# A transformer block's opening: the order of the first transfers, a column copy moved to another engine, and one more filling product

## The chip, the cores and the metric

The kernel runs on one core of one Trainium2 chip. The metric is the time of one execution on the device in microseconds (us), as the median of three runs. Besides the runs there is one execution that was taken with the hardware profiler; all rows below come from it.

## The reference, cut to what matters

The block takes x (512 rows of 1024 numbers), puts 16 meta rows ahead of it, normalizes every row, and projects the result with a wide matrix; two kinds of attention, gates, a merge and an output projection follow. The change touches only the first step and the transfers that stand beside it:

```python
h = jnp.concatenate([meta, x], axis=1)
h = layer_norm(h, emb_ln_g, emb_ln_b)
...
proj = jnp.einsum('bld,dn->bln', h, w_in[i])
```

`layer_norm` takes a row's mean and variance, then multiplies column by column by `emb_ln_g` and adds `emb_ln_b`. `b_gate` and `diff_subln_g` are small vectors that are used much later (a bias of the gates, the scale of a second norm).

## The kernel before, in words

The 512 rows of x are four tiles of 128 rows (`xts[0]` to `xts[3]`, here tile 0 to tile 3); the meta rows are a tile `mt` of 16 rows. For each tile the vector engine (DVE) takes statistics of the two halves of 512 columns (`stats`, line 323), joins them (line 327), and a reciprocal root follows: on ScalarE (ACT) for tile 0 (lines 329, 330), on GpSimd (POOL) for the others (lines 299, 300). DVE then writes the normalized tile (`norm_v`, line 340), except for the second half of tile 0, which ACT writes (`norm_s`, line 337). TensorE (PE) turns the tile by eight 128x128 transposes (`turn`, line 344). ACT scales and shifts each turned piece by the columns of `emb_ln_g` and `emb_ln_b` (`scaled`, line 384; two pieces of tile 0 go to DVE, line 386). As soon as a piece is there, PE multiplies it with the first weights (`query`, line 390: `x..` is the first weight block `raw0[:, 0]`, `y..` the second, `raw0[:, 1]`).

The columns themselves come from a transpose of 16 rows, `cp` (line 313), which PE makes after a run of filling products (`fill(WARM)`, lines 307 to 311; one filling product is two passes in the trace). The copy of `cp` out of PSUM into `cols` is line 415, in `norm0`, and it stands on ACT.

The order of the work of PE, DVE, ACT and POOL in this opening is written out by hand as a string and then pinned engine by engine (`keep_order`, line 970), so each engine does its work in the order of the text. Its first words are (`S` = statistics, `N` = normalize, `t` = turn, `F` = fill, `a` and `d` = scale on ACT and DVE):

```python
    def norm0():
        norm_v(0, X0)
        norm_s(0, X1)
        s.copy(cols[:, :16], av0[:, :16])
...
    order("""S0 norm0 t00 t01 t02 t03 S1 F2 a00 a01 a02 a03 a04 a05 d06 d07 x00 x01 x02 x03 x04 x05 N1 t10 t11 x06 x07 t12 t13
             a10 a11 a12 a13 a14 a15 a16 a17 S2 m0 m1 mr N2 S3 mnorm
             x10 y00 x11 y01 x12 y02 x13 y03 t20 more t21 t22 t23 x14 y04 x15 y05 x16 y06 x17 y07
```

The transfers into the chip are issued from SyncE (SP) in the order of lines 257 to 271: the halves of tile 0, the halves of tile 1, the two halves of the first weight block (`first_load`, line 133), tile 2, the second weight block, the meta rows, tile 3, the third weight block, `b_gate` and `diff_subln_g` into `rows2`, the fourth weight block, `diff_lambda`, and then the weights of the main part (`fetch`, line 145). The two vectors of the norm come on ACT's queue (lines 249, 250). Each transfer reports through a semaphore; SP has eight of them in turn, so a request waits until the one that last used its semaphore has landed.

Of the kernel before, what the change touches and what calls it, by code (L numbers as in the profile page):

```python
# [16 lines left out]
P = 128  # L17
# [17 lines left out]


ORDERED = [mybir.EngineType.PE, mybir.EngineType.DVE, mybir.EngineType.Activation, mybir.EngineType.Pool]
WARM = 12
SEVEN = 4
SUMS_AT = {0: [8.0], 1: [5.0, 11.0], 2: [8.0]}  # L40
TD = [(0.85, 11.0, 14.5), (0.95, 13.0, 16.5)]
# [5 lines left out]
def hybrid_block_kernel(ctx: ExitStack, tc: tile.TileContext, x, meta, emb_g, emb_b, w_in, b_gate,  # L47
                        diff_lambda, subln_g, w_br_d, w_br_s, w_out, ln_g, ln_b, out):
    nc = tc.nc
    v, s, g, pe = nc.vector, nc.scalar, nc.gpsimd, nc.tensor  # L50
# [22 lines left out]
    for u, (kind, n) in enumerate(UNITS):  # L73
        if u + 1 < len(UNITS):
            other, i = UNITS[u + 1]
# [15 lines left out]
    for n, (kind, i) in enumerate(seq):  # L91
        if kind in ("BD", "BS", "wd", "ws"):
# [6 lines left out]
            o = len(loads)  # L99
# [31 lines left out]
    def first_load(n, ks=slice(0, KT)):  # L131
        kind, i = seq[n]
        nc.sync.dma_start(raw0[:, n, ks], w_in[:, ks, ds(COL[kind] + i * P, P)])
# [118 lines left out]
    xts = [sp.tile([P, D], F32, name=f"xt{i}") for i in range(NB)]  # L252
# [1 line left out]
    mt = sp.tile([P, D], F32, name="mt")[:M]  # L254
    small = sp.tile([P, 512], F32, name="small")
    rows2, lamb = small[:17, :P], small[:, P:P + 256].rearrange("p (a d) -> p a d", a=4)
    for i in range(2):
        for o in (ts(0, 512), ts(1, 512)):
            nc.sync.dma_start(xts[i][:, o], x[0, ts(i, P), o])
    first_load(0, ts(0, 4))  # L260
    first_load(0, ts(1, 4))
    nc.sync.dma_start(xts[2], x[0, ts(2, P), :])
# [1 line left out]
    nc.sync.dma_start(mt, meta)  # L264
    nc.sync.dma_start(xts[3], x[0, ts(3, P), :])
    first_load(2)
    nc.sync.dma_start(rows2[0:16], b_gate[0].rearrange("a (k p) -> (a k) p", p=P))
    nc.sync.dma_start(rows2[16:17], subln_g)
    first_load(3)
    nc.sync.dma_start(lamb, diff_lambda[0].rearrange("a d -> (a d)").partition_broadcast(P))  # L270
    fetch(4)
# [14 lines left out]
    cols = const.tile([P, 33], F32, name="cols")  # L286
# [20 lines left out]
    def fill(count):  # L307
        for n in range(count):
            pe.matmul(warm, ident, ident, start=True, stop=True)

    fill(WARM)
    av0 = pav.tile([P, 512], F32, tag="av", name="cp")
# [23 lines left out]
    def norm_s(i, o):  # L336
        s.activation(xns[i][:, o], xts[i][:, o], AF.Identity, scale=xrs[:, i:i + 1], bias=nmr[i])

    def norm_v(i, o):
        v.tensor_scalar(xns[i][:, o], xts[i][:, o], xmv[:, i, 0:1], xrs[:, i:i + 1], op0=ALU.subtract, op1=ALU.mult)  # L340
# [71 lines left out]
    def norm0():  # L412
        norm_v(0, X0)
        norm_s(0, X1)
        s.copy(cols[:, :16], av0[:, :16])

    def mnorm():
        v.tensor_scalar(mn, mt, mmv[:, 0:1], mrs, op0=ALU.subtract, op1=ALU.mult)
# [33 lines left out]
    def lam2():  # L452
# [6 lines left out]
    steps["F"] = fill  # L459
    steps["H"], steps["L"] = lambda n, c: hi(2 * n + c), lambda n, c: lo(2 * n + c)  # L460
    words = dict(lam0=lam0, lam1=lam1, lam2=lam2, hm=lambda: s.copy(hTh[:, :, :M], hM), lm=low_meta, norm0=norm0, mnorm=mnorm, mturn=mturn, meta=meta, more=more_banks,
                 m0=lambda: stats(4, 0), m1=lambda: stats(4, 1), mr=lambda: rstd(4))

# [814 lines left out]
```

## Time and profile before

| | |
|---|---|
| median of three runs | 705.79 us (705.67 to 706.04) |
| the profiled execution's own time | 705.09 us |
| its span in the trace | 703.3 us |
| PE busy | 693.3 us, 99% of the span |
| DVE, ACT, POOL busy | 569.5, 440.5 and 129.8 us |

A row of a timeline gives the start and the length of a group of instructions from the start of the span, and in brackets how long its engine had been idle before it and who ended that idle time. `PEld` is the loading of the stationary operand of a matmul, which comes just ahead of the matmul. `SPq` and `ACTq` rows are the issue of a transfer, not the transfer. Matmul lengths overlap, since PE is pipelined: what counts for pace is the distance from one start to the next.

### The profile page before, as it was taken

How to read it: one execution, taken by the hardware profiler on the slowest of the kernel's cores; microseconds unless marked ns; L12 is line 12 of the kernel's file. 1: busy time of each engine (PE TensorE's matmuls, PEld its weight loads, DVE VectorE, ACT ScalarE, POOL GpSimd, SP SyncE). 2: the span in 40 equal slices, each digit the busy share in tenths (PEclk: the TensorE clock that was granted, in tenths of full speed). 3: DMA queues.
4: the chain of work that ended last, by engine and by line, in shares of the span. 5: the costliest groups of instructions: out<-in, count | busy, mean ns of one | idle time of the engine just before them, and what ended most of it. 6: DMA issues, size and time to landing. Idle time of an engine off the chain costs nothing.

```text
span 703.3 us, 13282 instructions
## 1 busy us (share of the span) xinstructions
PE 693.3 (99%) x4478; PEld 634.1 (90%) x4478; DVE 569.5 (81%) x1225; ACT 440.5 (63%) x1073; POOL 129.8 (18%) x140
## 2 busy tenths in 40 slices
PE   8999999999999999999999999999999999999996
PEld 8999999989899898999989899988888998999885
DVE  6887998878786777899887898977666888688887
ACT  6676767767566687777757687766555456555400
POOL 2243112222222201212121220000012201230011
PEclk9999999999999999999999999999999999999999
DMA  9399557988888796899898977547477749697702
GB/s 292 103 195 182 145 117 178 212 177 184 221 186 182 188 195 183 173 223 206 207 192 219 203 152 194 164 124 242 137 165 142 148 121 245 136 174 194 264 25 116
DMA packets 184215, 124.93 MB, mean 178 GB/s; under 512 B 8994, under 2 KB 168131, under 8 KB 184147
## 3 DMA queue, kind: packets, MB, share of 16 engines
q1 hardware_dynamic: 148050, 102.84, 50.5%
q0 software_dynamic: 35776, 20.19, 23.0%
q10 hardware_dynamic: 320, 1.06, 0.4%
q8 instruction: 35, 0.57, 0.3%
q14 instruction: 34, 0.27, 0.1%
HBM read 93.54 MB, written 9.44 MB: 146 GB/s over the span
## 4 chain that ended last, share of the span: by engine, by line
PE 93%; ACT 2%; SPq 1%; DVE 1%; DMA 1%; issue 0%; DVEq 0%; ACTq 0%
PE q L700 18%; PE ps L501 12%; PE ps L499 12%; PE ps L500 12%; PE q L1083 11%; PE pso L1206 6%; PE ps L515 6%; PE sc L764 6%; PE t L776 4%; PE tv L733 1%; PE av L931 1%; PE av L932 1%; DMA raw<-in_w_in_dram 1%; PE av L925 1%; PE av L933 1%; DMA xt<-in_x_dram 1%
## 5 line engine op out<-in xcount | busy, mean ns | idle before, releaser
L190 DVE TENSOR_TENSOR w<-raw,w 128x512 fp32r<-128x512 f32 x168 | 114.3, 689 | 37.7 <-ACT w L185 36.4
L500 PE MATMUL ps<-hTl,w 128*128 128x512 f32 x368 | 144.9, 394 | 0.0
L499 PE MATMUL ps<-hTh,w 128*128 128x512 f32 x368 | 144.7, 393 | 0.0
L501 PE MATMUL ps<-hTh,w 128*128 128x512 f32 x368 | 144.7, 393 | 0.0
L185 ACT CAST w<-raw 128x512 fp32r<-128x512 f32 x168 | 103.5, 627 | 11.6 <-PE ps L501 5.4
L147 POOL DMA_DIRECT2D rawk<-in_w_in_dram x48 | 66.1, 1630 | 119.5 <-DMA rawk<-in_w_in_dram 66.1
L700 PE MATMUL q<-tS,w 128*128 128x264 f32 x384 | 82.6, 289 | 0.0
L1083 PE MATMUL q<-gh,w 128*128 128x256 f32 x448 | 81.4, 283 | 0.2 <-ACT t L1092 0.2
L501 PEld LDWEIGHTS ps<-hTh,w 128*128 128x128 f32 x368 | 69.2, 188 | 13.5
L500 PEld LDWEIGHTS ps<-hTl,w 128*128 128x128 f32 x368 | 69.2, 188 | 13.1
L499 PEld LDWEIGHTS ps<-hTh,w 128*128 128x128 f32 x368 | 69.2, 188 | 13.0
L1083 PEld LDWEIGHTS q<-gh,w 128*128 128x128 f32 x448 | 70.2, 192 | 0.5 <-ACT t L1092 0.4
L764 PE MATMUL sc<-k,A 128*128 128x264 f32 (+3 forms) x320 | 66.0, 299 | 0.0
L700 PEld LDWEIGHTS q<-tS,w 128*128 128x128 f32 x384 | 63.7, 189 | 0.3
L1083 PE MATMUL q<-gl,w 128*128 128x256 f32 x224 | 63.5, 283 | 0.0
L700 PE MATMUL q<-hTh,w 128*128 128x264 f32 x288 | 60.8, 286 | 0.0
L916 DVE TENSOR_TENSOR_SCAN e<-e,diag 128x528 f32<-128x528 f32 (+1 forms) x64 | 54.2, 850 | 5.6 <-ACT e L910 5.6
L700 PE MATMUL q<-tl,w 128*128 128x264 f32 x192 | 54.9, 286 | 0.0
L764 PEld LDWEIGHTS sc<-k,A 128*128 128x128 f32 x320 | 50.1, 189 | 2.2
L515 PE MATMUL ps<-hTh,w 128*128 128x264 f32 x256 | 51.5, 289 | 0.2 <-ACT k L642 0.2
L700 PEld LDWEIGHTS q<-hTh,w 128*128 128x128 f32 x288 | 47.8, 189 | 1.0
L781 ACT CAST ah<-t 128x384 fp32r<-128x384 f32 (+2 forms) x72 | 34.3, 477 | 21.7 <-PE t L776 21.6
(284 smaller groups left out, 1572.1 us busy)
## 6 DMA issues: line engine op xcount, KB each, us to landing
raw<-in_w_in_dram SPq DMA_DIRECT2D x142, 256.0 KB, 3.4
rawk<-in_w_in_dram POOLq DMA_DIRECT2D x48, 256.0 KB, 5.7
rawk<-in_w_in_dram SPq DMA_DIRECT2D x36, 256.0 KB, 4.1
k<-ks SPq DMA_DIRECT2D x60, 132.0 KB, 3.0
raw<-in_w_out_dram SPq DMA_DIRECT2D x16, 256.0 KB, 4.0
k<-ks SPq DMA_DIRECT2D x60, 66.0 KB, 2.7
A<-low SPq DMA_DIRECT2D x28, 128.0 KB, 3.1
raw<-in_w_br_diff_dram SPq DMA_DIRECT2D x12, 256.0 KB, 3.3
```

The source lines that it names most:

```text
L147: second[l] = [lambda raw=raw, x=x: g.dma_start(raw, x, accum_op=ALU.add) for x in more]
L185: s.copy(wh, raw)
L190: eng.tensor_tensor(wl, raw, wh.bitcast(F32), op=ALU.subtract)
L499: pe.matmul(ps, wh[:, k % 4, :], hTh[:, k, M:], start=(k == 0), stop=False)
L500: pe.matmul(ps, wh[:, k % 4, :], hTl[:, k, M:], start=False, stop=False)
L501: pe.matmul(ps, wl[:, k % 4, :], hTh[:, k, M:], start=False, stop=(k == KT - 1))
L515: pe.matmul(ps[:, :H2], a[:, k % 4, :], b[:, k, ts(c, H2)], start=(k == 0 and m == 0), stop=(k == KT - 1 and m == 2))
L700: pe.matmul(bank, a[:, k, :], b, start=start and k == 0 and j == 0, stop=k == 3 and j == 2, skip_group_check=not start)
L764: pe.matmul(ps[:, :n], q, K[:, m, k0:k0 + n], start=(m == 0), stop=(m == 1))
L916: v.tensor_tensor_scan(rev, rev, diag[0][:, L - nk:][:, ::-1], 0.0, ALU.mult, ALU.max)
L1083: pe.matmul(bank, a[:, k, :], b[:, n, k, :], start=start and k == 0 and m == 0, stop=k == 3 and m == 2, skip_group_check=not start)
L1206: pe.matmul(ps, MH[k][:, ts(t, P)] if m == "h" else ML[:, k, ts(t, P)], WO[c]["hl".index(w)][:, k, r], start=(n == 0), stop=(n == 3 * KT - 1))
```

## The change

`WARM` goes from 12 to 13. Tile 1 is requested as a whole by one transfer in place of two halves. The requests for `b_gate` (16 rows of 128 numbers, 8 KB) and `diff_subln_g` (0.5 KB) move from behind the third weight block to a place ahead of the first weight block. The copy of the 16 columns goes from ACT to DVE, where it stands behind the normalization of tile 0's first half and ahead of the statistics of tile 1.

```diff
-WARM = 12
+WARM = 13
...
-    for i in range(2):
-        for o in (ts(0, 512), ts(1, 512)):
-            nc.sync.dma_start(xts[i][:, o], x[0, ts(i, P), o])
+    for o in (ts(0, 512), ts(1, 512)):
+        nc.sync.dma_start(xts[0][:, o], x[0, ts(0, P), o])
+    nc.sync.dma_start(xts[1], x[0, ts(1, P), :])
+    nc.sync.dma_start(rows2[0:16], b_gate[0].rearrange("a (k p) -> (a k) p", p=P))
+    nc.sync.dma_start(rows2[16:17], subln_g)
     first_load(0, ts(0, 4))
     first_load(0, ts(1, 4))
     nc.sync.dma_start(xts[2], x[0, ts(2, P), :])
@@
     nc.sync.dma_start(mt, meta)
     nc.sync.dma_start(xts[3], x[0, ts(3, P), :])
     first_load(2)
-    nc.sync.dma_start(rows2[0:16], b_gate[0].rearrange("a (k p) -> (a k) p", p=P))
-    nc.sync.dma_start(rows2[16:17], subln_g)
     first_load(3)
@@
     def norm0():
         norm_v(0, X0)
         norm_s(0, X1)
-        s.copy(cols[:, :16], av0[:, :16])
+        v.tensor_copy(cols[:, :16], av0[:, :16])
```

## Rows read from the trace of the kernel before

**Rows 1.** The page: busy time by engine; the chain that ended last.

```profile
PE 693.3 (99%) x4478; PEld 634.1 (90%) x4478; DVE 569.5 (81%) x1225; ACT 440.5 (63%) x1073; POOL 129.8 (18%) x140
...
PE 93%; ACT 2%; SPq 1%; DVE 1%; DMA 1%; issue 0%; DVEq 0%; ACTq 0%
```

**Rows 2.** Busy time by stretch: length, PE, PEld, DVE, ACT, POOL, clock, DMA share, GB/s.

```profile
5.97:7.15 1.18, 0.00 (x1) 0.00 (x1) 0.72 (x3) 0.86 (x3) 0.00 (x0) 1.00 1.11 342
...
10.27:26.27 16.00, 16.00 (x120) 15.02 (x118) 15.11 (x45) 13.93 (x38) 3.04 (x6) 1.00 0.68 210
...
34.00:703.30 669.30, 662.12 (x4257) 604.62 (x4255) 543.97 (x1156) 418.16 (x1015) 121.93 (x113) 1.00 0.75 177
```

**Rows 3.** Who waited for whom, on PE: us in total, times, longest.

```profile
PE bank L344 <- DVE xn L340: 1.2, 1, 1.2
```

**Rows 4.** Timeline of DVE, 0 to 22 us.

```profile
3.71 0.69 DVE L323 BATCH_NORM_STATS2 lnst<-xt 128x6 f32<-128x512 f32 x1 [1.91 <-DMA xt<-in_x_dram]
4.83 0.69 DVE L323 BATCH_NORM_STATS2 lnst<-xt 128x6 f32<-128x512 f32 x1 [0.43 <-DMA xt<-in_x_dram]
...
6.43 0.21 DVE L332 TENSOR_SCALAR nmr<-xmv,xrs 128x1 f32<-128x1 f32 x1 [0.66 <-ACT xrs L330]
6.56 0.54 DVE L340 TENSOR_SCALAR xn<-xt,xmv,xrs 128x512 f32<-128x512 f32 x1
7.01 1.28 DVE L323 BATCH_NORM_STATS2 lnst<-xt 128x6 f32<-128x512 f32 x2
...
9.54 1.00 DVE L340 TENSOR_SCALAR xn<-xt,xmv,xrs 128x512 f32<-128x512 f32 x2 [0.40 <-POOL xrs L300]
...
21.39 0.28 DVE L430 TENSOR_TENSOR hM<-bank,cols 128x128 f32<-128x128 f32 x1
21.71 0.29 DVE L431 TENSOR_TENSOR hM<-hM,cols 128x128 f32<-128x128 f32 x1
```

**Rows 5.** Timeline of PE's weight loads, 0 to 12 us; the last from 11.7 to 11.75.

```profile
7.15 0.85 PEld L344 LDWEIGHTS bank<-ident,xn 128*128 128x128 f32 x8 [1.27 <-DVE xn L340]
...
8.42 1.82 PEld L390 LDWEIGHTS bank<-hF,raw 128*128 128x128 f32 x12
10.15 0.47 PEld L344 LDWEIGHTS bank<-ident,xn 128*128 128x128 f32 x4
...
11.59 0.30 PEld L390 LDWEIGHTS bank<-hF,raw 128*128 128x128 f32 x2
```

**Rows 6.** Timeline of ACT, 0 to 22 us.

```profile
0.74 0.59 ACTq L249 DMA_DIRECT2D rows<-in_emb_ln_g_dram  x1
...
7.40 0.15 ACT L415 COPY cols<-cp 128x16 f32<-128x16 f32 x1
7.69 2.20 ACT L384 ACTIVATE hF<-bank,cols 128x128 f32<-128x128 f32 x6
```

**Rows 7.** Timeline of SP's queue, 0 to 22 us.

```profile
0.74 1.82 SPq L259 DMA_DIRECT2D xt<-in_x_dram  x4
2.60 0.98 SPq L133 DMA_DIRECT2D raw<-in_w_in_dram  x2
...
4.18 0.43 SPq L133 DMA_DIRECT2D raw<-in_w_in_dram  x1
4.82 2.36 SPq L264 DMA_DIRECT2D mt<-in_meta_tokens_dram  x1
...
8.16 1.94 SPq L267 DMA_DIRECT2D small<-in_b_gate_dram  x1
10.14 0.31 SPq L268 DMA_DIRECT2D small<-in_diff_subln_g_dram  x1
```

**Rows 8.** Issues around 2.3, 3.3 and 4.4 us: size, us from issue to landing.

```profile
xt<-in_x_dram SPq DMA_DIRECT2D x1, 256.0 KB, 5.0
...
raw<-in_w_in_dram SPq DMA_DIRECT2D x1, 256.0 KB, 5.5
...
raw<-in_w_in_dram SPq DMA_DIRECT2D x1, 512.0 KB, 7.4
```

## The prediction, made before the changed kernel was run

> **What bounds the kernel now.** I read the page first. PE is busy for 693.3 of 703.3 us, and the chain that ended last is 93% PE [rows 1]: what the opening does to the time is what it does to the moment from which PE runs without a gap. So I looked for that moment in the table of stretches [rows 2]. From 5.97 to 7.15 us PE does nothing; from 10.27 to 26.27 it is busy for 16.00 of 16.00 us; behind 34 us for 662.12 of 669.30. A delay ahead of 10.27 us therefore goes through to the end nearly whole, and a gain too, since hardly any idle time is left to take it up. The list of waits says the same: behind the first filling products, PE waits long in the opening only once, 1.2 us for the normalized first half of tile 0 [rows 3].
>
> The next step is what sets 10.27 us. PE's loads [rows 5] show the first six products in twelve loads from 8.42 us, and then at 10.15 us the first transpose of tile 1. That transpose has two conditions: the sixth product ahead of it in PE's order, and DVE's normalized half of tile 1. DVE writes that half from 9.54 us, 0.54 us for a half by tile 0's row, so until 10.08 us [rows 4]. Tile 0 shows how long the hand-over to PE takes: the half ends at 6.56 + 0.54 = 7.10 us and PE loads at 7.15. So 10.08 plus 0.05 is 10.13, and PE loads at 10.15: DVE's chain has no slack worth the name here, and neither have the products. The chain back from there is DVE's and POOL's: the half waited 0.40 us for POOL's root, POOL for the statistics of tile 1, and these started at 7.01 us directly behind tile 0's half, with no idle time noted [rows 4].
>
> **The change, part by part.**
>
> *One filling product more* is two passes. Eight loads take 0.85 us [rows 5], some 0.11 us from one to the next, so it adds 0.22 us to PE ahead of the transpose of the columns. PE is idle from 5.97 to 7.15 us [rows 2], which hides it; without that cover it would cost its 0.22 us. The columns would be there at about 6.2 us, and the copy can't start on DVE before 7.0. The granted clock is 1.00 in that stretch, the higher of the two levels, so there is no lower clock to be avoided. Zero.
>
> *The column copy leaves ACT.* It ran from 7.40 to 7.55 us, and the first scaled piece started at 7.69 [rows 6]. That piece also needs the first two transposes, which were loaded from 7.15 us [rows 5]. So ACT gains between 0 and 0.15 us, and I take 0.05. It reaches PE as a sixth product that ends sooner by as much. But the transpose behind it has its other condition at 10.13 us, and that one does not come sooner. The gain is hidden: zero.
>
> *The column copy goes to DVE*, behind tile 0's half and ahead of the statistics of tile 1. Queued behind it are the statistics, the joining, POOL's root, the normalization of tile 1 and the transposes. The trace has no such copy on DVE. The lower bound is a small instruction on operands outside PSUM: from 6.43 to 6.56 us, 0.13 us from start to start. The upper bound is an instruction that reads 128 columns from PSUM: from 21.39 to 21.71 us, 0.32 us [rows 4]. Sixteen columns are nearer to the small one; with a little for the PSUM read I take 0.15 us. The copy's own input has long been there, so it adds no wait. No gain is possible from this item, as DVE has no idle time there to fall into.
>
> [...]
>
> *Tile 1 requested whole.* SP saves one issue, 1.82 / 4 = 0.46 us [rows 7]. The fourth request was issued at about 0.74 + 3 x 0.47 = 2.15 us and landed 5.0 us later, at 7.1 [rows 7, 8]. Before, the first statistics needed only the third request; now they need the whole tile. The bytes and their place in the queue are the same, so I take 7.1 again. DVE comes to them at 7.01 + 0.15 = 7.16 us, so there is 0.06 us of slack. Landing sooner gains nothing, as DVE is busy; landing later costs its lateness. Zero, with a small margin.
>
> *The small requests ahead of the first weights.* Issuing 8 KB with nothing queued should cost SP what ACT's first request of 4 KB cost, 0.59 us at most [rows 6], and the 0.5 KB took 0.31 [rows 7]. Less the saved 0.46 us the first weights are issued up to 0.44 us later; I take 0.25. Their second half was issued at 2.60 + 0.48 = 3.08 us and landed 5.5 us later, at 8.6 [rows 7, 8]. Its first user is the fifth product, the ninth of the twelve loads from 8.42 to 10.24, at about 9.6 us [rows 5]. A slack of 1.0 us covers it. The second weight block is tighter: issued at 4.18, landed 7.4 us later, at 11.6 [rows 7, 8], and needed by the second load of the pair from 11.59, after the two of a first-weight product, at 11.70 [rows 5]. With DVE's delay it is needed at 11.85. The DMA engines are full meanwhile (share 1.11 at 342 GB/s, [rows 2]), so it lands by the bytes ahead of it: 8.5 KB more are 0.025 us. By bytes it lands at 11.63, by issue at 11.85, both in time. Zero.
>
> *Behind the third weight block* SP loses two issues, 1.94 and 0.31 us [rows 7]. The fourth block and the rest are then requested up to 2.3 us sooner. Nothing in PE's gapless 16 us waited for them, so that is worth nothing.
>
> **The sum** is +0.15 us, with 0.13 and 0.32 as the bounds of its one term. Against the profiled execution it is 705.09 + 0.15 = 705.24. That execution was 0.70 us below the median of the runs, so on the runs' scale I forecast 705.79 + 0.15 = 705.94, given as 705.9. A measurement of this kernel can tell about 0.2% from no change, 1.41 us: faster is below 704.38, slower above 707.20. So the forecast is no change that can be told.
>
> **The rivals.**
>
> *A: tile 0 lands sooner.* DVE waited 0.43 us for the second half of tile 0 and 1.91 us for the first [rows 4]. Fewer, larger requests behind it could let the second half through sooner. For it: these waits are on the path, ahead of everything. Against it: both requests stand ahead of every changed one in SP's order. Full success on the second half gives 0.15 - 0.43 = -0.28, 705.5 us. With some of the 1.91 us as well the gain could pass 1.41.
>
> *B: tile 1 lands later as a whole.* It decides from 7.16 us on, microsecond for microsecond. If the whole lands 0.5 us later than its second half did, the time is 705.79 + 0.15 + 0.44 = 706.4 us. For it: the slack is 0.06 us. Against it: same bytes, same place.
>
> *C: the small requests carry their long issue with them*, and the weights come late: the slower side. The two slow issues in the list are small ones, 2.36 us for 64 KB and 1.94 us for 8 KB [rows 7]. If 1.94 is the price of such a request wherever it stands, the weights are issued 1.94 + 0.31 - 0.46 = 1.8 us later. Where they land by issue, the second weight block lands at 11.6 + 1.8 = 13.4 instead of 11.6, and PE, which needs it at 11.70, stands for 1.7 us: 705.79 + 1.7 = 707.5 us, slower by 0.24%. It decides from a landing behind 11.85 us. For it: both rows. Against it: both stood directly behind a 512 KB request with more than 1 MB under way, whereas the 0.5 KB request took 0.31 and ACT's 0.59; and the engines were full, so that a later issue must not mean a later landing.
>
> *D: the copy costs nothing after all*, since the hand-over to the next instruction overlaps. Then nothing moves: 705.8 us.
>
> **How the numbers follow.** The forecast, with its bounds up to 0.32 us, has a chance of 0.60; A 0.14, most of it at a few tenths; B 0.11; C 0.10, of which 0.07 passes 1.41 us; D 0.05. Beyond 1.41 us faster there is only the far end of A, 0.03. So faster 0.03, slower 0.07, same 0.90. The range reaches from A's 705.5 less what the runs scatter (0.12 and 0.25 us about their median), 705.2, to B's 706.4 plus the same and a little for C's lighter forms, 706.8. Left out are C's full price and A's far end, under 2 in 10.
>
> **What would show it.** Right: a DVE copy of some 0.15 us from start to start at about 7.0 us; the statistics of tile 1 at 7.1 to 7.2; the first transpose of tile 1 at about 10.3; PE without a gap from there; the fill and the transpose of the columns done by 6.3 us. The step on ACT is right if its first piece starts hardly before 7.65 us. Wrong: an idle time of DVE ahead of tile 1's statistics that a transfer ended (B); statistics of tile 0 that start before 3.7 or 4.8 us (A); a long issue of `b_gate` at 2.1 us and PE waiting for weights at 8.4 or 11.7 us (C). A time outside 705.2 to 706.8 with this opening intact would mean that the order of later transfers changed the main part, which nothing in these rows lets me price.

## The result, and the profile after

The kernel after takes 706.62 us, median of its runs (705.85 to 707.72), the kernel before 705.76 beside it (704.66 to 706.30). The ratio is 1.0015, 95% interval 1.0009 to 1.0021: slower by 1.06 us by the ratio (0.86 by the two medians). That is less than the 1.41 us that the prediction took as what can be told, but the interval lies wholly above 1. The forecast was 705.9, in the range 705.2 to 706.8. The profiled execution took 706.10 us with a span of 704.3; that of before took 705.09 with 703.3, so the two traces differ by the same 1.0 us.

The page of the kernel after, as in [rows 1], and two stretches, as in [rows 2]; the last line is the second of these in the kernel before.

```profile
PE 694.4 (99%) x4480; PEld 635.0 (90%) x4480; DVE 570.5 (81%) x1226; ACT 440.7 (63%) x1072; POOL 129.8 (18%) x140
```

```profile
10.27:26.27 16.00, 16.00 (x118) 15.01 (x118) 15.12 (x45) 13.87 (x38) 3.04 (x6) 1.00 0.66 202
26.27:34.00 7.73, 7.18 (x56) 6.82 (x55) 5.26 (x13) 3.27 (x10) 3.06 (x10) 1.00 0.28 82
```

```profile
26.27:34.00 7.73, 7.51 (x59) 7.17 (x58) 5.21 (x13) 3.58 (x11) 3.12 (x10) 1.00 0.28 79
```

PE is gapless from 10.27 us in both. Then the kernel after loses 0.33 us against the kernel before between 26 and 34 us (7.18 us busy in place of 7.51), where the prediction looked for nothing.

The opening of the kernel after: DVE's timeline, as in [rows 4], then PE's, then the loads, as in [rows 5], then SP's queue, as in [rows 7].

```profile
3.42 0.69 DVE L323 BATCH_NORM_STATS2 lnst<-xt 128x6 f32<-128x512 f32 x1 [1.63 <-DMA xt<-in_x_dram]
4.75 0.69 DVE L323 BATCH_NORM_STATS2 lnst<-xt 128x6 f32<-128x512 f32 x1 [0.63 <-DMA xt<-in_x_dram]
...
6.48 0.54 DVE L340 TENSOR_SCALAR xn<-xt,xmv,xrs 128x512 f32<-128x512 f32 x1
6.98 0.17 DVE L415 COPY cols<-cp 128x16 f32<-128x16 f32 x1
7.08 1.29 DVE L323 BATCH_NORM_STATS2 lnst<-xt 128x6 f32<-128x512 f32 x2
...
9.62 1.00 DVE L340 TENSOR_SCALAR xn<-xt,xmv,xrs 128x512 f32<-128x512 f32 x2 [0.42 <-POOL xrs L300]
```

```profile
1.43 5.35 PE L309 MATMUL warm<-ident 128*128 128x128 f32 x26 [1.43 <-POOL ident masks.py:199]
6.71 0.23 PE L313 MATMUL cp<-ident,rows 16*128 16x16 f32 x1
```

```profile
8.34 1.76 PEld L390 LDWEIGHTS bank<-hF,raw 128*128 128x128 f32 x12
10.22 0.42 PEld L344 LDWEIGHTS bank<-ident,xn 128*128 128x128 f32 x4
```

```profile
1.66 0.42 SPq L259 DMA_DIRECT2D xt<-in_x_dram  x1
2.12 0.43 SPq L260 DMA_DIRECT2D small<-in_b_gate_dram  x1
2.59 0.33 SPq L261 DMA_DIRECT2D small<-in_diff_subln_g_dram  x1
2.96 0.95 SPq L133 DMA_DIRECT2D raw<-in_w_in_dram  x2
...
4.74 0.37 SPq L133 DMA_DIRECT2D raw<-in_w_in_dram  x1
```

The copy stands where it was forecast, at 6.98 us, and the statistics of tile 1 start 0.10 us behind its start. The first transpose of tile 1 is loaded at 10.22 us, 0.07 later than before; the first product of L515 (the first step of the main part) begins, counted from its weight load, at 26.26 us against 26.24. So the opening gave away 0.02 us of the 1.02.

**Where the 1.02 us are.** I lined up the starts of all products of both traces. The distance between them is 0.02 us until 33 us, then jumps to 0.39 at one product of L515, and stays 0.39 to the last product, at 696.42 us against 696.03. Behind that the kernel after needs 7.91 us to its end, the kernel before 7.28: 0.63 more. 0.02 + 0.37 + 0.63 = 1.02.

**The jump at 33 us.** The list of waits on PE from 26 to 36 us, first after, then before; and below it ACT's timeline there, after and before.

```profile
PE ps L515 <- ACT k L642: 0.5, 1, 0.5
```

```profile
PE ps L515 <- ACT k L642: 0.2, 1, 0.2
```

```profile
30.88 0.38 ACT L637 CAST k<-ps 64x264 fp32r<-64x264 f32 x1 [3.37 <-DVE sides L600]
```

```profile
30.50 0.37 ACT L637 CAST k<-ps 64x264 fp32r<-64x264 f32 x1 [3.03 <-DVE nlam L453]
```

L637 is the first copy of keys out of PSUM, and PE needs it. Both copies wait for DVE's `nlam` (a small column, line 453), which ends at 30.40 after and 30.34 before. Before, the copy starts 0.16 us behind it, after, 0.48. The four wait instructions that belong to the copy (times in ns: least, median, longest) say where the rest is, after and before:

```profile
L637 ACTq EVENT_SEMAPHORE  x4: 17/38/2989, 27.3 to 30.8; - x4
```

```profile
L637 ACTq EVENT_SEMAPHORE  x4: 38/38/2648, 27.3 to 30.4; - x4
```

ACT stands still for 0.35 us ahead of its 64th record in both: a *stand*, a stretch in which an engine does nothing and nothing that the profile shows holds it. Before, that record is the long wait itself: ACT's 63rd record ends at 27.38, the long wait begins only at 27.73 and is shorter for it, 2.65 us. After, ACT has one instruction fewer in the opening, the column copy. The long wait is its 63rd record, 2.99 us, and the stand falls behind it, from 30.44 to 30.80, when `nlam` has come and nothing hides it: the copies that follow, L642 last, come later by as much, and PE waits for that one. The releaser in brackets, `sides`, has no part in it: before, `sides` ends at 30.78, and the copy has started at 30.50.

**The longer end.** SP's waits for the last two requests of the output (in all, times, longest), after and before; then the DMA view over 2.5 us from 0.12 us behind the last request, 40 slices of 0.0625 us, after and before.

```profile
SPq L1273 <- DMA out_dram<-hr: 1.7, 2, 1.1
```

```profile
SPq L1273 <- DMA out_dram<-hr: 1.1, 2, 0.6
```

```profile
GB/s 328 295 426 492 492 328 360 426 426 262 131 131 361 360 393 459 393 295 360 492 426 328 164 33 33 0 33 33 33 0 0 0 0 0 0 0 0 0 0 0
...
q14 instruction: 1, 0.01, 1.0%
```

```profile
GB/s 33 295 393 492 426 295 393 492 426 360 393 230 328 393 459 459 360 360 426 492 393 328 132 33 0 0 0 0 0 0 0 0 0 0 0 0 0 0 0 0
```

33 GB/s in a slice is one packet of 2 KB. Before, the last packets end together. After, an 8 KB packet of instructions lies among them (it takes 0.41 us), and packets of 2 KB come one by one for 0.4 us more. The request's semaphore says the same: it takes 16 steps, which before all come 1.85 to 2.00 us behind the request; after, 15 come by 1.99 and the sixteenth at 2.48. I read this as one of the 16 DMA engines that fell behind by about the length of the instruction packet. That packet moved at 697.7 us before, ahead of the last outputs, and at 701.8 after. What calls the packet is in no record; if it is tied to a count of SP's records, as I take it, it comes one instruction later in the kernel after, since SP has one request fewer (864 records in place of 865). From the records: the last request is issued 0.09 us later behind a stand of SP of 0.33 us, its landing takes 2.50 us in place of 2.02, and one wait of 0.06 us more follows: 0.63.

### The profile page after: what moved, and what is told of

Its sections match the earlier page's. It is cut to its first block, busy times and chain, and to the rows that moved or that the text cites. A ratio compares the mean times of both kernels' runs of the same rounds, so it can differ in the third digit from the quotient of the medians.

```text
span 704.3 us, 13284 instructions
## 1 busy us (share of the span) xinstructions
PE 694.4 (99%) x4480; PEld 635.0 (90%) x4480; DVE 570.5 (81%) x1226; ACT 440.7 (63%) x1072; POOL 129.8 (18%) x140
## 3 DMA queue, kind: packets, MB, share of 16 engines
q10 hardware_dynamic: 320, 1.06, 0.4%
## 4 chain that ended last, share of the span: by engine, by line
PE 93%; DVE 3%; ACT 2%; DMA 1%; issue 0%; POOL 0%; DVEq 0%; SPq 0%; POOLq 0%; ACTq 0%
PE q L700 18%; PE ps L499 12%; PE ps L501 12%; PE ps L500 12%; PE q L1083 11%; PE pso L1206 6%; PE ps L515 6%; PE sc L764 6%; PE t L776 4%; PE tv L733 1%; DVE lnst L323 1%; PE av L931 1%; PE av L932 1%; PE av L925 1%; PE av L933 1%; DMA xt<-in_x_dram 1%
## 5 line engine op out<-in xcount | busy, mean ns | idle before, releaser
L764 PE MATMUL sc<-k,A 128*128 128x264 f32 (+3 forms) x320 | 66.0, 299 | 0.0
L764 PEld LDWEIGHTS sc<-k,A 128*128 128x128 f32 x320 | 50.1, 189 | 2.2
L515 PE MATMUL ps<-hTh,w 128*128 128x264 f32 x256 | 51.5, 288 | 0.5 <-ACT k L642 0.5
```

The costliest lines, as they stand in the source:

```text
L515: pe.matmul(ps[:, :H2], a[:, k % 4, :], b[:, k, ts(c, H2)], start=(k == 0 and m == 0), stop=(k == KT - 1 and m == 2))
L764: pe.matmul(ps[:, :n], q, K[:, m, k0:k0 + n], start=(m == 0), stop=(m == 1))
```

## The experiments

Three theories stood against each other. **P**: the loss is in the engines' stands, and these lie at fixed counts of each engine's instructions, so that an instruction taken out puts a stand in another place of the program, far away. **C**: the columns are late, because the fill is slow, and DVE waits for them. **R**: the requests' new order itself costs.

One table of all traces first; the parts of the time are from the start to the first product of L515 (its weight load), from there to the last product, and from there to the end, in us. "Wait" is the longest wait ahead of L637, in us, which tells on which side the stand lies (2.65 ahead of it, 2.97 behind). An interval of 0.0009 to either side is 0.6 us, so no time in the last column tells two terms of 0.4 and 0.6 us apart by itself; the traces do.

| kernel | SP's records | wait | start | middle | end | ratio to before |
|---|---|---|---|---|---|---|
| before | 865 | 2.65 | 26.24 | 669.79 | 7.28 | |
| after | 864 | 2.99 | 26.26 | 670.16 | 7.91 | 1.0015 [1.0009, 1.0021] |
| e1, copy back | 864 | 2.67 | 26.29 | 670.67 | 7.89 | 1.0008 [0.9999, 1.0017] |
| e2, copy alone | 865 | 2.96 | 26.26 | 670.43 | 7.29 | 1.0002 [0.9993, 1.0011] |
| e3, one copy on ACT | 864 | 2.97 | 26.38 | 670.28 | 7.89 | 1.0012 [1.0003, 1.0020] |
| e4, 12 fills | 864 | 2.98 | 26.26 | 670.86 | 7.89 | 1.0009 [1.0000, 1.0017] |
| f1, two copies on ACT | 864 | 2.66 | 26.51 | 670.25 | 7.90 | 1.0012 [1.0003, 1.0021] |
| f2, halves | 865 | 2.96 | 27.66 | 670.76 | 7.29 | 1.0017 [1.0008, 1.0026] |
| f3, halves and two copies | 865 | 2.65 | 27.14 | 670.30 | 7.28 | 1.0011 [1.0002, 1.0019] |
| f4, two more requests | 866 | 2.96 | 26.71 | 670.73 | 7.74 | 1.0021 [1.0012, 1.0031] |
| h1, a late request | 865 | 2.98 | 26.20 | 670.22 | 7.28 | 1.0004 [0.9995, 1.0014] |
| h2, all three | 865 | 2.67 | 26.31 | 669.81 | 7.28 | 0.9999 [0.9990, 1.0009] |
| h3, whole tile alone | 864 | 2.65 | 26.84 | 670.27 | 7.89 | 1.0007 [0.9998, 1.0016] |
| i1, before again | 865 | 2.65 | 26.46 | 669.85 | 7.29 | 0.9998 [0.9989, 1.0007] |

No trace is an exception: the end is 7.89 to 7.91 in the six with 864 records of SP and 7.28 to 7.29 in the seven with 865, and the wait is 2.65 to 2.67 wherever ACT has its old count ahead of L637, 2.96 to 2.99 wherever it has one fewer.

**e1, the copy back on ACT.**

```diff
-        v.tensor_copy(cols[:, :16], av0[:, :16])
+        s.copy(cols[:, :16], av0[:, :16])
```

> The changed kernel with the column copy back on ACT (new requests and 13 filling products stay). Theory P, a pause of ACT: ACT stands for about 0.35 us ahead of the same instruction by count; in the kernel before it stood there from 27.38 to 27.73 us, ahead of its long wait for DVE, so that it was hidden; with one instruction fewer it stands there behind that wait, from 30.44 to 30.80, and the first key copy and all that follows on PE come 0.39 us later. P expects here the first key copy at about 30.5 us (changed kernel 30.88), PE's last matmul 0.35 to 0.4 us sooner than in the changed kernel, and a time between the two, near +0.5 us over the kernel before. Theory C, late columns: the columns' transpose stands behind 26 passes of filling, most of them at the lower clock, and DVE waits for it in some executions; C expects that loss gone too. Theory R, the requests: the new order of the transfers makes the time longer; R expects no gain, +1.0 us over the kernel before.

The stand is back ahead of the long wait (2.67), and L637 starts 0.15 us behind `nlam`. The step at 33 us shrinks from 0.37 to 0.13 us; that rest is `nlam`'s, which ends 0.12 us later behind the first product of L515 than before. The end stayed at 7.89. The time is 0.0008 over before, but PE's last product did not come sooner than in the kernel after, as P expected: it came at 696.96 us against 696.42, since PE lost 0.27 us at 402 us and 0.50 at 492 (for these steps see i1).

**e2, the copy alone: the kernel before with the copy on DVE.**

```diff
-        s.copy(cols[:, :16], av0[:, :16])
+        v.tensor_copy(cols[:, :16], av0[:, :16])
```

> The kernel before with nothing but the column copy moved from ACT to DVE (12 filling products, old requests). P expects the pause behind the long wait, the first key copy at about 30.9 us and PE's last matmul 0.4 us later than before: +0.4 to +0.5 us with the copy's 0.1 us on DVE. C expects little beyond the copy's 0.1 us, as there are only 24 passes ahead of the columns. R expects no more than the copy's own 0.1 us.

The stand is behind the wait (2.96), and PE loses 0.43 us at 33 us. With the requests of before the end is 7.29. So the two losses have two causes: the step goes with the copy, the end with the requests. The time can't be told from before; its interval holds both no loss and the 0.4 us that P expected.

**e3, one small copy on ACT in the opening.**

```diff
-    fill(WARM)
+    fill(WARM); extra = sp.tile([P, 16], F32, name="extra"); s.copy(extra, ones[:, :16])
```

> The changed kernel with one small copy more on ACT (16 columns, not used by anything), early, while ACT is idle. It gives ACT its old count of instructions and leaves everything else of the change. P expects the pause ahead of the long wait again: the first key copy at about 30.5 us, PE's last matmul 0.35 to 0.4 us sooner than in the changed kernel, time about 0.4 us below it. C and R expect no difference from the changed kernel: first key copy at 30.9 us, +1.0 us over the kernel before.

It missed: the stand stayed behind the wait. The records say why. The new copy took over a wait for which the kernel after has an instruction of its own (ahead of L329), so ACT had as many records as without it. The count had not been changed, and P was not tested; f1 does it.

**e4, twelve filling products.**

```diff
-WARM = 13
+WARM = 12
```

> The changed kernel with 12 filling products again. C expects that the columns are ready one product sooner (0.2 to 0.4 us), DVE's copy at once behind tile 0's half, and a mean time some tenths of a us below the changed kernel, more where the higher clock comes late. P and R expect no change from the changed kernel: first key copy at about 30.9 us, +1.0 us over the kernel before.

The columns' transpose starts at 6.38 us and is done at 6.61, the copy stands at 7.00 and waits for nothing. Nothing of the loss changed: stand behind the wait, end 7.89. The extra product is the cause of neither part.

**f1, two small copies on ACT.**

```diff
+    ... s.copy(extra[:, :16], ones[:, :16]); s.copy(extra[:, 16:], ones[:, :16])
```

> The kernel after, with two small copies of 16 columns on ACT in the opening instead of none. The one extra copy tried before added no record, because it took over the wait of an instruction that had stood by itself; two add one net, so that ACT has as many records ahead of the first key copy (L637) as in the kernel before. If ACT's pause of 0.35 us lies at a fixed count of its instructions, it is back ahead of the long wait for nlam, L637 starts at 30.5 to 30.6 and not at 30.9, and the step of 0.4 us in PE at 33 us is gone; the end, from the last matmul on, stays at 7.9 us. Time 0.4 us below the kernel after, so about 0.5 above the kernel before. If the pause belongs to the copy's being on DVE (late columns, or DVE being behind), L637 stays at 30.9 and the time stays at 0.9 to 1.0 us above before.

P's part is as expected: the wait is 2.66, L637 starts 0.15 us behind `nlam`, and the step at 33 us is gone, with the copy still on DVE. The time did not fall with it, since PE lost 0.47 us at 492 us in this execution, and since C's case came too. DVE's timeline:

```profile
6.26 0.54 DVE L340 TENSOR_SCALAR xn<-xt,xmv,xrs 128x512 f32<-128x512 f32 x1
7.25 0.17 DVE L415 COPY cols<-cp 128x16 f32<-128x16 f32 x1 [0.45 <-PE cp L313]
7.34 1.27 DVE L323 BATCH_NORM_STATS2 lnst<-xt 128x6 f32<-128x512 f32 x2
```

The columns came at 7.22 us, DVE stood 0.45 us for them, and tile 1's first transpose came at 10.47. So C is real as well. In the kernel after it cost 0.05 us: there the columns are done at 6.94, the copy starts 0.04 us behind them as it does here, and it stands 0.50 us behind the start of tile 0's half, where it is 0.45 when the columns are early (e2, e4, f4).

**f2, tile 1 in halves again**, the small requests still first.

```diff
-    nc.sync.dma_start(xts[1], x[0, ts(1, P), :])
+    for o in (ts(0, 512), ts(1, 512)): nc.sync.dma_start(xts[1][:, o], x[0, ts(1, P), o])
```

> The kernel after, with tile 1 asked for in two halves again: the small requests stay ahead of the weights, the copy stays on DVE, WARM stays 13; SP has as many requests as in the kernel before. If the longer end comes of SP having one request fewer (the 8 KB block of SP's instructions is then fetched while the last output is being written, and one of the 16 DMA engines ends 0.4 to 0.5 us after the others), the end from the last matmul on is 7.3 us and not 7.9, no instruction packet stands among the last output's, and the time is 0.6 us below the kernel after, 0.4 above the kernel before. If the order of the small requests lengthens the end, it stays at 7.9 us and the time within 0.1 us of the kernel after. L637 stays at 30.9 in both.

The end is 7.29 with no instruction packet in it: SP's count, not the order, as P has it. But the time did not fall, for a reason that no theory had. PE's loads:

```profile
11.73 0.30 PEld L390 LDWEIGHTS bank<-hF,raw 128*128 128x128 f32 x2
13.12 0.95 PEld L390 LDWEIGHTS bank<-hF,raw 128*128 128x128 f32 x6 [1.09 <-DMA raw<-in_w_in_dram]
```

The second weight block was issued at 5.21 us, 0.47 later than in the kernel after, and PE stood 1.09 us for it. In the kernel after, PE does not wait for it.

**f3, halves and two copies on ACT** (the edits of f1 and f2).

> Both at once: tile 1 in two halves and two small copies on ACT; the small requests ahead of the weights, the norm columns' copy on DVE and WARM 13 stay. If the two counts are the whole loss, the end is 7.3 us, L637 starts at 30.5 to 30.6, and the time is within 0.15 us of the kernel before although all that the change meant to do is still in it but for the whole tile. If the opening itself lost time, it stays 0.4 us or more above the kernel before.

End 7.28 and wait 2.65, both as expected; the time is not: PE stood 0.66 us for the same weight block, and lost 0.53 us at 492 us.

**f4, tile 1 and tile 3 in halves** (the edit of f2, and this).

```diff
-    nc.sync.dma_start(xts[3], x[0, ts(3, P), :])
+    for o in (ts(0, 512), ts(1, 512)): nc.sync.dma_start(xts[3][:, o], x[0, ts(3, P), o])
```

> The kernel after, with tile 1 and tile 3 each in two halves: one request more than the kernel before, two more than the kernel after, so that the rotation of the DMA semaphores stands one step off the kernel before on the other side. If only the place at which SP's instructions are fetched counts, the fetch falls one instruction earlier than in the kernel before, ahead of the last outputs, and the end is 7.3 us. If the rotation of the semaphores lengthens the end, it is 7.5 us or more. L637 stays at 30.9. Time by the first 0.4 above the kernel before, by the second 0.6 to 1.0.

No packet in the end, and the last output lands as early as before; still the end is 7.74. At the end SP waits for one DMA semaphore after another (before, from 700.84 us on, 0.06 us from one to the next). In this kernel the last request has an early one, and seven waits of 0.06 us follow it. So both hold: the count decides about the packet (0.5 us), the rotation about how many waits follow (0.06 us each; one of them in the kernel after).

**h1, one late request more**: the last tile's rows for the residual, at 660 us, in halves. The opening is that of the kernel after.

```diff
-        nc.sync.dma_start(hrs[t], x[0, ts(t, P), :])
+        for o in ([ts(0, 512), ts(1, 512)] if t == NB - 1 else [ds(0, D)]): nc.sync.dma_start(hrs[t][:, o], x[0, ts(t, P), o])
```

> The kernel after with one request more at 660 us, where nothing waits: the rows of the last tile for the residual are asked for in two halves. The whole opening stays as changed. If the longer end is a matter of SP's count of requests alone, the end from the last matmul on is 7.3 us, no instruction packet stands among the last output's, and the time is 0.6 us below the kernel after, 0.3 to 0.5 above the kernel before. If the opening's order makes the end longer, it stays at 7.9.

The end is 7.28. The DMA view, as for after and before above:

```profile
GB/s 33 295 393 492 426 328 426 426 492 393 295 295 295 361 459 492 360 360 426 459 393 328 132 33 0 0 0 0 0 0 0 0 0 0 0 0 0 0 0 0
```

The last packets end together again. One request at 660 us took back the 0.63 us that one request at 2 us had cost. The ratio is 1.0004; its interval holds both no loss and the 0.3 to 0.5 us that were expected.

**h3, the whole tile alone** in the kernel before.

```diff
-        for o in (ts(0, 512), ts(1, 512)):
+        for o in (ts(0, 512), ts(1, 512)) if i == 0 else (ds(0, D),):
```

> The kernel before with tile 1's rows asked for whole and nothing else: SP has one request fewer, the small requests keep their late place, the copy stays on ACT, WARM 12. If SP's count sets the end, it is 7.9 us here too, with an instruction packet among the last output's, and the time is 0.5 to 0.6 us above the kernel before, though the opening is as before. If the small requests' new place were the reason, the end stays at 7.3 and the time within 0.1 us of the kernel before. L637 stays at 30.5.

One request fewer, and the end is 7.89, the small requests being where they always were. That is the count from the other side. The opening did not stay as before: PE stood 0.35 us for the second weight block, as in f2, and the start is 0.60 us longer.

**h2, all three taken back**: the edits of h1 and f1, and the columns' transpose after six filling products.

```diff
-    fill(WARM)
+    fill(6)
...
-    pe.transpose(av0[:, :16], rows, ident[:16, :16])
+    pe.transpose(av0[:, :16], rows, ident[:16, :16]); fill(WARM - 6)
```

> The kernel after with all three losses taken back, and nothing of its opening: the late request in two halves (SP's count), two small copies on ACT in the opening (ACT's count), and the norm columns' transpose put after the sixth filling product instead of after the thirteenth (columns ready by 4.5 us, so DVE's copy never waits for the fill). Expected: columns transposed by 4.5, copy at 7.0, first transpose of tile 1 at 10.2, L637 at 30.5 to 30.6, end 7.3. If these are all of the loss, the time is within 0.2 us of the kernel before (+0.1 the forecast's own copy). If something else of the change costs, it is 0.4 or more above. It is below the kernel before only if the tile asked for whole brings something, for which no trace speaks.

PE's and DVE's timeline and the waits of L637:

```profile
4.29 0.28 PE L313 MATMUL cp<-ident,rows 16*128 16x16 f32 x1
```

```profile
6.66 0.17 DVE L415 COPY cols<-cp 128x16 f32<-128x16 f32 x1
7.14 1.29 DVE L323 BATCH_NORM_STATS2 lnst<-xt 128x6 f32<-128x512 f32 x2 [0.31 <-DMA xt<-in_x_dram]
```

```profile
L637 ACTq EVENT_SEMAPHORE  x4: 17/38/2668, 27.3 to 30.5; - x4
```

The columns no longer hold the copy, the stand is ahead of the wait, the end is 7.28: start, middle and end are each within 0.07 us of before, and so is the time (0.9999, with an interval that ends at 1.0009, where that of the kernel after begins). All parts of the change are in this kernel. By the trace nothing of it is left that costs more than 0.09 us of span, and nothing that gains: here the copy ended ahead of tile 1's landing, and DVE stood 0.31 us for the tile.

**i1, the kernel before again**, as control.

> The kernel before once more, unchanged, as its own control. Between the first key copy and the end, the traces of the changed kernels show two further steps in PE, of 0.2 to 0.5 us, at 402 us (L764) and at 492 us (L926), in some executions and not in others; the execution of the kernel before that was read first shows neither, and stands 0.7 us below the median of its runs. If these steps come and go from one execution to the next, this execution may show one or both, with the end at 7.3 us and L637 some 4.25 us after the first product of L515 as before, and the ratio is 1.000 within its interval. If they belong to the changed kernels, neither shows here.

The end is the same, the start 0.22 us longer, the ratio 0.9998. The steps that lengthen "middle" in other kernels, 0.2 to 0.4 us at 402 us (L764: e1, e2, e4, h3) and 0.2 to 0.7 us at 492 us (L926: e1, e3, e4 and f1 to f4), do not show here at 402, and with 0.15 us at 492, where the first trace of the same program has none. The kernel after has neither, so they have no part in the 1.02 us of its trace. Whether the larger ones belong to a program or to an execution is open, and so is how much of them is in the medians. No version beat both kernels: h2 is the kernel before in time.

## Why the prediction was right and wrong

**The opening was right.** The copy at 6.98 us, tile 1's statistics at 7.08, PE gapless from 10.2 us, no long issue of the small requests (0.43 and 0.33 us), so C of the rivals did not come. The copy cost 0.10 us from start to start where 0.15 was taken; its own record lasts 0.17 us. The statistics of tile 1 still stand 0.15 us further behind tile 0's half than before (0.60 against 0.45), but 0.05 of that is the wait for the columns, where the prediction had said that the copy "adds no wait": the figure came out by luck. Tile 0 landed 0.07 us sooner in this execution, which hid part of it.

**The step that failed is the sum with one term.** Two items in it were set to zero after their local time alone had been looked at. *"The column copy leaves ACT"* was worth nothing because the piece behind it gains at most 0.15 us that PE can't use. ACT did gain 0.14 (its first piece at 7.55, not 7.69) where 0.05 was taken, some 0.08 of it by tile 0's sooner landing, and PE could not use it. But the copy is also one of the 63 records ahead of ACT's stand, and without it the stand moved from before a wait to behind it: +0.37 us. *"SP saves one issue"* was counted at 0.46 us of issue time; it is also one of SP's 865 records, and without it the instruction packet came into the last output: +0.63. The prediction's last sentence named the main part as what it couldn't price, but blamed the order of later transfers, and that did not change. With both terms the sum is 0.15 + 0.37 + 0.63 = 1.15, against 1.02 in the traces and 1.06 by the ratio. That the median of 706.62 us lies inside the range is luck: its upper end was put there for B, a later tile 1, which did not come.

**A cover was thinner than told.** The extra filling product was costed at nothing since the columns "would be there at about 6.2 us". They came at 6.94, 0.04 us ahead of the copy. The pace of the fill is what varies: the fill's products by stretch (length, PE and PEld with the number under way, granted clock, DMA share, GB/s), in the kernel before, then after.

```profile
3.50:4.50 1.00, 1.00 (x7) 1.00 (x6) 1.00 0.67 193
4.50:5.50 1.00, 1.00 (x11) 1.00 (x10) 1.00 0.90 273
```

```profile
3.50:4.50 1.00, 1.00 (x7) 1.00 (x6) 1.00 0.80 295
4.50:5.50 1.00, 1.00 (x7) 1.00 (x6) 1.00 0.80 280
```

From start to start a pass of the fill takes 0.21 us at first and 0.11 us later, half of it. The faster pace comes at 4.5 us before and at 6.0 after, and there the trace's first record of the clock begins, a grant of 1.00: at 4.48 us before, 6.04 after, and 7.56 in i1, with before's own program, so the moment shifts from one execution to the next without any change. PE had been filling from 1.43 us on in all three. Ahead of its first record the trace says nothing of the clock; the column prints 1.00 there too, in three of these four stretches. The only other grant in the two traces is 0.50, and it stands behind PE's last product (700.9 to 703.3 us before, 699.0 to 704.3 after). Half the pace would fit it, though no record says so. The sentence that there is "no lower clock to be avoided" holds for the stretch in which it was read, 5.97 to 7.15 us before, where the grant is 1.00; the first passes of the fill, at half the pace, have no record of the clock. ACT's copy at 7.40 did not mind. On DVE, in front of tile 1's chain, a late column is on the path: 0.05 us in the kernel after, and in f1 0.25 us more at the start.

**A second cover held, but not as told.** The second weight block was issued at 4.74 us, 0.56 later than before, where 0.25 was taken. It had become SP's ninth request, and took the semaphore of the second half of tile 0, which landed at 4.73. It landed at 11.55 all the same, 0.07 sooner than before, and PE did not wait.

**The rivals.** B's margin was 0.02 us where 0.06 was told: tile 1 landed at 7.06, DVE came at 7.08. A's sign is in the trace, statistics of tile 0 at 3.42 and 4.75 us, but it is not the change's: the second half of tile 0 landed between 4.62 and 4.87 us in the three traces with the old requests, and between 4.52 and 5.00 in the eleven others. None of the four named what happened.

## What to carry to other kernels

Here an instruction or a request that was taken out of an engine's stream moved everything behind it by one place, while the engine's stand stayed at its count (ACT's 64th record, SP's 848th) and so fell on another instruction. So ask of each removed instruction where the next stand lies in that engine's records, and whether it passes from in front of a long wait to behind it; in these traces a stand is a hole of 0.35 us (ACT) or 0.33 us (SP) that nothing released. If a small change costs some tenths far from where it was made, add a harmless instruction or request back at a place where nobody waits, and see whether the time returns.

## What was not expected of the hardware

Stands at a fixed count: in all 14 traces ACT stands 0.35 us ahead of its 64th record, wherever that is. SP has one of 0.33 us ahead of its 848th record: in the six traces with 864 records it lies between the last two requests of the output (700.46 to 700.80 after), in f4 inside a long wait. In the seven with 865 records the 848th is itself the request that waits 4.0 us for DVE, and hides it. That these stands belong to the loading of instructions is my inference, and no record shows it: behind each, one 8 KB packet of the kind "instruction" moves, 0.6 to 1.0 us behind the end of ACT's in all 14 traces (27.73 before, a packet at 28.7) and 1.0 us behind SP's in the six (700.80 after, a packet at 701.8). Packets of 8 KB (33 in the span after) stand beside packets of 16 KB (35). What the traces show of their cost: a stand was hidden only where the engine waited anyway. Where it was not, it cost 0.37 us at one place, and 0.5 us went with one packet among the last output's.

The second weight block is late when either half of the request change is made alone (PE stands 0.35 us for it in h3, 0.62 to 1.09 in f2 to f4), and in time with both. In f2 to f4 a part is in the record: tile 2 is SP's ninth request there and waits for the semaphore of tile 0's second half (issued at 4.82 us in f2, landing at 4.81), and the weight block comes behind it as the tenth. In h3 the block was issued at 3.70 us, sooner than in any other kernel, and landed at 12.26; why is open.
